# A hybrid decoder trunk on one core: half-precision pairs in the input projection from the second block on, and one small product in two halves

## The chip, the cores and the metric

The kernel runs on one core of one Trainium2 chip, as one launch. The metric is its device time in microseconds: 3231.13 us before the change, the median of three runs (3227.33 to 3232.68).

The core has five engines with queues of their own: TensorE (PE, its weight loads shown apart as PEld), VectorE (DVE), ScalarE (ACT), GpSimd (POOL) and SyncE (SP, which here only issues DMAs).

## What is computed

Two layers over 2048 tokens of width 1024, both with a pre-RMSNorm and a residual: a Mamba-2 mixer, then latent attention. The change touches the Mamba-2 mixer alone:

```python
proj = h @ w_in                                   # (2048, 1024) @ (1024, 5152)
z, xBC, dt_raw = jnp.split(proj, [D_INNER, D_INNER + CONV_DIM], axis=-1)
xBC = jax.nn.silu(causal_depthwise_conv(xBC, conv_w, conv_b))
xs, Bm, Cm = jnp.split(xBC, [D_INNER, D_INNER + SSM_GROUPS * SSM_STATE], axis=-1)
dt = jax.nn.softplus((dt_raw + dt_bias).astype(jnp.float32))
...
y_intra = jnp.einsum('btsg,btsgh,bsgh,bsghp->btghp', CB, L, dt_c, x_c)
y_inter = jnp.einsum('btgn,bghpn,btgh->btghp', C_c, state, jnp.exp(cum))
...
y = y.reshape(Bsz, S, D_INNER) * jax.nn.silu(z.astype(jnp.float32))
```

`h` is the normalised input; `L` are the decays inside a chunk. 32 heads of 64 channels in 4 groups, a state of 128, float32 in and out.

## The kernel before

**Tiling.** The tokens go in 4 blocks `b` of 512 (`TB`), the 32 heads in 4 groups `g` of 8; a block has 4 chunks `c` of 128 tokens. The width of 1024 is 8 tiles `k` of 128 rows (`KD`).

**Three matmuls for a product.** Operands of large products are kept as a pair, high part and rest, each in fp32r. `mm3` (lines 85 to 87) adds high x high, high x low and low x high. `split` (108 and 109; with a scale 111 and 112) makes such a pair: ACT copies into the high part, DVE subtracts. `pair16` (116 and 117) does the same in float16 and is used in the attention part.

**The projection of a pair (b, g).** `xbc` has two sweeps, B and C (2 banks) and x (4 banks); `zgate` has one (4 banks). Each takes 8 weight tiles from memory (`wraw`, three buffers), splits each (`wsp`, six buffers) and issues the three matmuls of 512 columns per bank and tile. So the weights are loaded and split anew in each block. `prep` turns the normalised input by PE transposes (line 171) and splits it into `xT`; `steps` makes the step sizes dt, with their own small weights (line 427).

**The scan of a pair (b, g).** `ssd` goes through 4 chunks: a transpose and a product for B and C, the decays (`E`, tile `big`, times the masked product), `Xd` = x times dt, then eight fp32 matmuls `E x Xd`, one for each head (line 549), then the state's part (`Ct` with the old state `Sp`), the new state (`Bt` with `Xp`), the gate and the turn into `yT`. The low halves of Xp, Ct and Sp are subtracted on POOL (line 500). `outp` multiplies `yT` with the output weights.

**Order.** `mamba` interleaves: while the scan of (b, g) runs, PE gets the output product of the pair before and the projection of the pair after, cut into pieces between which the scan's steps are drawn. The last group but one of a block also brings `prep` and `steps` of the next block. A scheduler then orders the instructions of each engine; weight preparation is drawn ahead by a priority (`AHEAD`).

Of the kernel before, what the change touches and what calls it, by code (L numbers as in the profile page):

```python
# [20 lines left out]
P = 128  # L21
T = 2048
D = 1024
# [45 lines left out]
class Net:  # L69
# [54 lines left out]

    def wunit(self, src, n, scale=None, late=False):

        with self.tc.high_priority(AHEAD):
            raw = self.raw(late)
            self.nc.sync.dma_start(raw[:, :n], src)
            if late:  # L130
                self.turn = not self.turn
                w = [self.t(self.sp, f"st{2 * self.turn + i}", [P, TB], F32R, bufs=1) for i in range(2)]
            else:
                u = self.t(self.wp, "wsp", [P, 2, TB], F32R, bufs=WSP)
                w = [u[:, i, :] for i in range(2)]
            self.split(w[0][:, :n], w[1][:, :n], raw[:, :n], scale)
        return w

# [47 lines left out]
    def layer_constants(self, cp):  # L186
# [13 lines left out]
        nc.vector.memset(self.mk[:, P:], NEG)  # L200
        self.wdt = cp.tile([P, KD, 2, H], F32R, name="wdt")
        self.split(self.wdt[:, :, 0], self.wdt[:, :, 1], wdt[:, :KD * H].rearrange("p (k c) -> p k c", k=KD))
# [21 lines left out]
    def mamba(self, cp):  # L224
# [9 lines left out]
        for n, (b, g) in enumerate(items):  # L234
# [81 lines left out]
    def prep(self, b, gain=None, tag="tr", each=4):  # L316
# [3 lines left out]
        for k in range(KD):  # L320
# [4 lines left out]
            if k % each == each - 1:  # L325
                yield

    def xbc(self, b, g):

        nc, w_in, xT = self.nc, self.a["ssm_w_in"], self.xT[b]  # L330
        outs = []
        for chans, tag, bufs in (([16 + g, 20 + g], "BC", 4), ([4 * g + j for j in range(4)], "xs", 8)):
            banks = [self.t(self.pp, "mm", [P, TB], bufs=4) for _ in chans]

            def weights(k):
                rows = slice(k * P, (k + 1) * P)
                if tag == "xs":
                    return self.wunit(w_in[rows, DI + g * 512:DI + (g + 1) * 512], 512)
                both = w_in[rows, DI + DI:DI + DI + 1024].rearrange("p (n q c) -> p n q c", n=2, q=G)
                with self.tc.high_priority(AHEAD):  # L340
                    raw = self.t(self.wp, "wraw", [P, TB], bufs=WRAW)
                    nc.sync.dma_start(raw[:, :256].rearrange("p (n c) -> p n c", n=2), both[:, :, g, :])
                    w = self.t(self.wp, "wsp", [P, 2, TB], F32R, bufs=WSP)
                    w = [w[:, n, :256] for n in range(2)]
                    self.split(*w, raw[:, :256])
                return w
# [24 lines left out]
    def zgate(self, b, g):  # L371

        nc, xT = self.nc, self.xT[b]
        banks, out = [self.t(self.pp, "mm", [P, TB], bufs=4) for _ in range(4)], []

        def weights(k):
            return self.wunit(self.a["ssm_w_in"][k * P:(k + 1) * P, g * 512:(g + 1) * 512], 512)

# [4 lines left out]
        def evacuate(bank, i):  # L383
            sz = self.t(self.sp, "sz", [P, TB], bufs=SZ)
            nc.scalar.activation(sz, bank, AF.Tanh, scale=0.5)
            nc.vector.scalar_tensor_tensor(sz, sz, 1.0, bank, ALU.add, ALU.mult)
            out.append(sz)
# [32 lines left out]
    def steps(self, b):  # L420

        nc, v, xT = self.nc, self.nc.vector, self.xT[b]
        ps = self.t(self.pp, "tr", [P, TB], bufs=4)

        for k in range(KD):
            for n in range(2):
                nc.tensor.matmul(ps[0:2 * H, :], self.wdt[:, k].rearrange("p n h -> p (n h)"), xT[k][:, n, :],
                                 start=k + n == 0, stop=k + n == KD)
        wk = self.t(self.sp, "big", [P, D], bufs=2)
        rt = self.t(self.sp, "yt", [2 * H, TB], bufs=2)  # L430
        nc.scalar.activation(rt, ps[0:2 * H, :], AF.Copy)
        ps = self.t(self.pp, "tr", [P, TB], bufs=4)
# [50 lines left out]
    def ssd(self, b, g):  # L483
# [21 lines left out]
        for c in range(4):  # L505
# [41 lines left out]
            for h in range(8):  # L547
                hc = slice(h * 64, (h + 1) * 64)
                nc.tensor.matmul(yi[:, hc], E[:, h, :], Xd[:, hc], start=True, stop=True)  # L549
            v.tensor_tensor(y, y, yi, ALU.add)  # L550
# [19 lines left out]
            yield  # L570
            v.tensor_tensor(y, y, szs[c], ALU.mult)
            junk = self.t(self.sp, "yt", [P, TB], bufs=2)
# [546 lines left out]
    def run(self):  # L1119
        tc = self.tc  # L1120
        with ExitStack() as whole:
# [72 lines left out]
```

## Time and profile before

| | |
|---|---|
| median of three runs | 3231.13 us |
| profiled execution | 3232.49 us |
| its span | 3230.7 us |
| Mamba-2 part, first chunk to last (86.8 to about 1620 us) | about 1530 us |
| a pair (b, g) | 83 to 113 us |

The profile is of one execution. A row of a group reads: line of the kernel, engine, operation, tile written <- tiles read, shape, count, then busy time in us and the mean duration in ns, then the engine's idle time ahead of it. A matmul's recorded duration is longer than its share of PE's time, since the next one starts before it ends; what a matmul costs in a row of them is the time from start to start (its pitch). `128*128` is the part of the array that it uses (rows * columns). One fp32 matmul stands as two, one for each of its passes.

### The profile page before, as it was taken

What the parts mean: (1) busy time and instruction counts of PE and PEld (TensorE: products, weight loads), DVE (VectorE), ACT (ScalarE), POOL (GpSimd) and SP (SyncE); (2) the same over time, 40 slices, a digit from 0 to 9 for tenths busy, and PEclk for the clock granted to TensorE, in tenths of its full rate; (3) what the DMA queues carried; (4) which work ended last, traced back from release to release, by engine and by line L of the source; (5) the groups of instructions that cost most, each with busy time, mean ns of one, the idle gap of its engine ahead of it and who ended that gap; (6) DMA issues with size and microseconds to landing.
All of it is one profiled execution on the core that took longest, in us unless ns stands there. A gap on an engine that the chain in (4) does not pass through costs nothing.

```text
span 3230.7 us, 50468 instructions
## 1 busy us (share of the span) xinstructions
PE 3152.1 (98%) x16708; PEld 2559.6 (79%) x16708; DVE 2597.2 (80%) x5490; ACT 2058.5 (64%) x5115; POOL 641.7 (20%) x846
## 2 busy tenths in 40 slices
PE   8999999999999999999999999999999999999998
PEld 6788888888888888788888888777777777777787
DVE  6888888888889888888876765678888888888675
ACT  5666666656567666576655554567777778778522
POOL 1221112221222212222111211222212221222100
PEclk9999999999999999999999999999999999999999
DMA  5333334333433334333466666854443534444385
GB/s 174 106 98 97 119 122 132 100 92 122 142 98 102 97 114 146 124 106 104 129 229 213 234 206 206 247 135 81 84 80 78 100 76 89 79 89 113 83 279 164
DMA packets 210054, 418.90 MB, mean 130 GB/s; under 512 B 27104, under 2 KB 68832, under 8 KB 208352
## 3 DMA queue, kind: packets, MB, share of 16 engines
q1 hardware_dynamic: 168032, 290.34, 29.4%
q0 software_dynamic: 41760, 125.34, 16.0%
q8 instruction: 132, 2.16, 0.3%
q14 instruction: 130, 1.06, 0.1%
HBM read 321.33 MB, written 94.24 MB: 129 GB/s over the span
## 4 chain that ended last, share of the span: by engine, by line
PE 58%; DVE 10%; ACT 4%; DMA 3%; issue 2%; SPq 0%; POOL 0%; ACTq 0%; DVEq 0%
PE mm L85 11%; PE mm L87 11%; PE mm L86 11%; PE tr L937 6%; PE tr L947 3%; PE tr L948 3%; PE tr L85 3%; PE tr L86 3%; PE tr L87 3%; DVE cacc L362 2%; PE tr L549 2%; DVE wsp L109 1%; ACT Pr L922 1%; DMA os<-ri_d 1%; DVE big L528 1%
## 5 line engine op out<-in xcount | busy, mean ns | idle before, releaser
L117 DVE SCALAR_TENSOR_TENSOR PTs<-tr,PTs 128x512 f16<-128x512 f32 (+3 forms) x640 | 374.7, 607 | 93.9 <-ACT PTs L116 87.7
L116 ACT ACTIVATE PTs<-tr 128x512 f16<-128x512 f32 (+3 forms) x640 | 328.6, 541 | 140.2 <-PE tr L937 139.4
L910 DVE TENSOR_REDUCE mx<-mm 128x1 f32<-128x512 f32 (+2 forms) x631 | 375.4, 607 | 45.4 <-PE mm L87 42.7
L922 ACT ACTIVATE Pr<-mm,nm 128x512 f32<-128x512 f32 (+2 forms) x631 | 395.4, 636 | 23.1 <-DVE nm L914 21.4
L108 ACT ACTIVATE wsp<-wraw 128x512 fp32r<-128x512 f32 (+1 forms) x452 | 252.1, 574 | 173.6 <-PE mm L87 77.4
L109 DVE TENSOR_TENSOR wsp<-wraw,wsp 128x512 fp32r<-128x512 f32 (+1 forms) x452 | 301.1, 678 | 68.0 <-ACT wsp L108 67.7
L85 PE MATMUL mm<-xT,wsp 128*128 128x512 f32 x800 | 321.2, 402 | 0.0
L937 PE MATMUL tr<-pack,Pr 128*128 128x128 f32 x2176 | 317.5, 273 | 2.0 <-ACT Os L954 1.9
L87 PE MATMUL mm<-xT,wsp 128*128 128x512 f32 x800 | 313.9, 392 | 0.0
L86 PE MATMUL mm<-xT,wsp 128*128 128x512 f32 x800 | 313.3, 392 | 0.0
L85 PE MATMUL mm<-K,xT 96*128 96x512 f32 (+2 forms) x639 | 286.7, 449 | 23.7 <-ACT Pr L922 22.7
L937 PEld LDWEIGHTS tr<-pack,Pr 128*128 128x128 f32 x2176 | 253.3, 141 | 50.4 <-ACT Os L954 2.7
L85 PE MATMUL mm<-wsp,xT 128*128 128x512 f32 (+1 forms) x640 | 242.4, 379 | 0.1
L86 PE MATMUL mm<-wsp,xT 128*128 128x512 f32 (+1 forms) x640 | 237.8, 372 | 0.0
L87 PE MATMUL mm<-wsp,xT 128*128 128x512 f32 (+1 forms) x640 | 237.5, 372 | 0.0
L87 PE MATMUL mm<-K,xT 96*128 96x512 f32 (+2 forms) x639 | 231.6, 362 | 0.0
L86 PE MATMUL mm<-K,xT 96*128 96x512 f32 (+2 forms) x639 | 231.1, 362 | 0.0
L362 DVE SCALAR_TENSOR_TENSOR cacc<-craw,pack,cacc 128x512 f32<-128x512 f32 x288 | 217.4, 776 | 16.6 <-ACT cacc L360 16.0
L542 ACT ACTIVATE Xw<-tr,d_wend 128x64 f32<-128x64 f32 x512 | 183.4, 359 | 66.0 <-DVE Xd L538 57.5
L500 POOL TENSOR_TENSOR Xp<-Xw,Xp 128x512 fp32r<-128x512 f32 x64 | 83.0, 1297 | 708.2 <-ACT Xp L499 426.0
L947 PE MATMUL tr<-PTs,xT 128*128 128x512 f16 (+3 forms) x640 | 222.0, 348 | 0.1
L948 PE MATMUL tr<-PTs,xT 128*128 128x512 f16 (+3 forms) x640 | 219.4, 347 | 0.0
(370 smaller groups left out, 8139.5 us busy)
## 6 DMA issues: line engine op xcount, KB each, us to landing
wraw<-in_ssm_w_in_dram SPq DMA_DIRECT2D x256, 256.0 KB, 2.8
big<-cumT SPq DMA_DIRECT2D x64, 512.0 KB, 4.3
wraw<-in_ssm_w_out_dram SPq DMA_DIRECT2D x128, 256.0 KB, 2.6
wraw<-in_ssm_w_in_dram SPq DMA_DIRECT2D x129, 128.0 KB, 2.3
xT<-qn_d POOLq DMA_DIRECT2D x64, 256.0 KB, 4.5
K<-kn_d POOLq DMA_DIRECT2D x15, 1024.0 KB, 9.3
wraw<-in_mla_w_uq_dram SPq DMA_DIRECT2D x36, 256.0 KB, 4.5
hx<-in_x_dram SPq DMA_DIRECT2D x16, 512.0 KB, 4.8
```

The lines of the kernel that those rows point to most:

```text
L85: mm(out, l_hi, r_hi, start=start, stop=False)
L86: mm(out, l_hi, r_lo, start=False, stop=False)
L87: mm(out, l_lo, r_hi, start=False, stop=stop)
L109: nc.vector.tensor_tensor(lo, src, hi.bitcast(F32), ALU.subtract)
L116: self.nc.scalar.activation(hi, src, AF.Copy, scale=scale)
L117: self.nc.vector.scalar_tensor_tensor(lo, src, scale, hi, ALU.mult, ALU.subtract)
L362: nc.vector.scalar_tensor_tensor(acc, raw[:, k:k + TB], wk[k], acc, ALU.mult, ALU.add)
L910: v.tensor_reduce(mx[:, n:n + 1], s[:, :w], AX.X, ALU.max)
L922: nc.scalar.activation(x[:, :w], s[:, :w], AF.Exp, bias=nm, accum_out=sm[:, n:n + 1])
L937: nc.tensor.transpose(pt[:, j * P:(j + 1) * P], st["P"][j][kb], self.ident)
L947: nc.tensor.matmul(st["O"][:, c], vals[h][:, kb, :], u[:, 0], start=kb == 0, stop=False)
L948: nc.tensor.matmul(st["O"][:, c], vals[h][:, kb, :], u[:, 1], start=False, stop=kb == nk - 1)
```

## The change

**Half-precision pairs.** In block 0 the projection stays as it was, and while its weights go by, the sum of squares of each weight row is taken: an ACT Square with a row sum ahead of each split (`dt_norm` does it for the dt columns on DVE). `row_scale` makes a power of two for each row of the weights (`rw`) and the matching gain for the input (`xg`), with one factor for the whole (`un`, `unh`) that brings the products back. From block 1 on, `prep16` writes the input, and `wpair` the weights, as float16 pairs, two tiles `k` in one buffer. In block 1 `wpair` makes them from the loaded weights and stores them to memory (`w16_d`); in blocks 2 and 3 it only loads them. `dt_pair` does the same for the dt weights. The evacuations multiply by `un` or `unh`, and so does the gate in the scan.

At the end of block 0 the output product moves behind the projection, and `row_scale` stands ahead of `prep16`.

**The product inside a chunk.** Each of the eight `E x Xd` matmuls is issued as two, with 64 columns of `E` each, which write partitions 0 to 63 and 64 to 127.

```diff
+            if norm is not None:
+                self.nc.scalar.activation(w[1][:, :n], raw[:, :n], AF.Square, accum_out=norm)
             self.split(w[0][:, :n], w[1][:, :n], raw[:, :n], scale)
...
+    def wpair(self, b, g, at, n, k, src):
+        nc = self.nc
+        if k % 2 == 0:
+            with self.tc.high_priority(AHEAD):
+                u = self.w16 = self.t(self.wp, "wsp", [P, 2, 2, n], F16, bufs=WSP)
+                kept = self.w16_d[k * P:(k + 2) * P, g, at:at + 2 * n].rearrange(
+                    "(j p) (s c) -> p j s c", j=2, s=2)
+                if b == 1:
+                    for j in range(2):
+                        raw = self.t(self.wp, "wraw", [P, TB], bufs=WRAW)
+                        src(k + j, raw)
+                        self.pair16(u[:, j, 0], u[:, j, 1], raw[:, :n], self.rw[:, k + j:k + j + 1])
+                    nc.gpsimd.dma_start(kept, u)
+                else:
+                    nc.sync.dma_start(u, kept)
+        u = self.w16
+        return [u[:, k % 2, i, :] for i in range(2)]
...
+    def row_scale(self):
...
+        v.tensor_reduce(n, self.nrm, AX.X, ALU.add)
...
+        nc.tensor.transpose(ps[0:1, 0:P], m, self.ident)
...
+        nc.tensor.matmul(ps[:, 0:2], self.ones[0:1, :], r, start=True, stop=True)
...
+    def dt_pair(self, b):
...
+                self.pair16(w[:, k, 0], w[:, k, 1], raw[:, k * H:(k + 1) * H], self.rw[:, k:k + 1])
+            nc.gpsimd.dma_start(self.wdt_d, w.rearrange("p k n h -> p (k n h)"))
...
-                parts += [self.prep(b + 1, self.g0), self.steps(b + 1)]
+                if b == 0:
+                    parts = parts[1:] + parts[:1] + [self.row_scale()]
+                parts += [self.prep16(b + 1), self.steps(b + 1)]
                 total += 3
+            elif b == 0 and g == 1:
+                self.dt_norm()
...
+    def prep16(self, b):
...
+            if k % 2 == 0:
+                u = self.t(self.xq, "xT", [P, 2, 2, TB], F16, bufs=8)
+            w = u[:, k % 2]
+            self.pair16(w[:, 0, :], w[:, 1, :], ps, self.xg[:, k:k + 1])
...
+                if b:
+                    return self.wpair(b, g, 1024 if tag == "xs" else 2048, n, k, load)
...
+                    nc.scalar.activation(w[1], raw[:, :n], AF.Square, accum_out=self.nrm[:, k, at:at + 1])
...
-                nc.scalar.activation(raw[:, 3:], bank, AF.Copy)
+                nc.scalar.activation(raw[:, 3:], bank, AF.Copy, scale=self.un if b else 1.0)
...
+            if b:
+                return self.wpair(b, g, 0, 512, k, load)
...
-                nc.tensor.matmul(yi[:, hc], E[:, h, :], Xd[:, hc], start=True, stop=True)
+                for t in (slice(0, 64), slice(64, P)):
+                    nc.tensor.matmul(yi[t, hc], E[:, h, t], Xd[:, hc], start=True, stop=True)
...
-            v.tensor_tensor(y, y, szs[c], ALU.mult)
+            if b:
+                v.scalar_tensor_tensor(y, y, self.un, szs[c], ALU.mult, ALU.mult)
+            else:
+                v.tensor_tensor(y, y, szs[c], ALU.mult)
```

Three places in the order of instructions. First PE, in the middle of a chunk of block 1, before the change: the projection's last matmuls, the decays times `Xd` (eight fp32 matmuls in one row), the state's part, and the projection again.

```order
L85 MATMUL mm_5925<-xT_3570,wsp_6009 128x512
L86 MATMUL mm_5925<-xT_3570,wsp_6009 128x512
L87 MATMUL mm_5925<-xT_3570,wsp_6009 128x512
L549 MATMUL tr_6021<-Xd_5976,big_5942 128x64 x8
L85 MATMUL tr_6031<-Sp_5860,Ct_5950 128x512
L86 MATMUL tr_6031<-Sp_5860,Ct_5950 128x512
L87 MATMUL tr_6031<-Sp_5860,Ct_5950 128x512
L85 MATMUL mm_5924<-xT_3578,wsp_6040 128x512
```

And such a place after it:

```order
L87 LDWEIGHTS wsp_6321
L87 MATMUL mm_6250<-xT_3798,wsp_6321 128x512
L683 MATMUL tr_6346<-Xd_6301,big_6267 64x64 x16
L85 MATMUL tr_6364<-Sp_6185,Ct_6275 128x512
L86 MATMUL tr_6364<-Sp_6185,Ct_6275 128x512
L87 MATMUL tr_6364<-Sp_6185,Ct_6275 128x512
L85 LDWEIGHTS wsp_6371
L85 MATMUL mm_6249<-xT_3824,wsp_6371 128x512
```

The eight matmuls have become sixteen of 64x64 in the same place, the two halves of a head behind each other; the float16 weight loads have rows of their own, which fp32r loads had not.

Second PE, at the end of block 0 after the change, around the two PE steps of `row_scale` (`rm`, a column of maxima, turned; `rr`, the factors, spread over all partitions). Between the first two and the last three rows lie matmuls of the output product like those shown.

```order
L87 MATMUL tr_3739<-Xp_3673,Bt_3578 128x512
L200 MATMUL tr_3761<-pack,rm_3759 1x128
L85 MATMUL mm_3964<-wsp_3970,yT_2960 128x512
...
L87 MATMUL mm_3964<-wsp_4058,yT_2960 128x512
L210 MATMUL tr_3771<-rr_684_3763,ones 128x2
L264 MATMUL tr_3778<-pack,hx_2709 128x128
```

The scale's two steps on PE stand 25 matmuls of the output product apart, and behind the second one come the transposes of block 1's input.

Third POOL, in block 0's last group, where the projection of block 1 begins, after the change (`w_d` is the store of pairs).

```order
L633 TENSOR_TENSOR Xp_4297<-Xw_4256,Xp_4297 128x512
L483 COPY halo<-craw_4372 128x3
L483 COPY halo<-craw_4401 128x3
L633 TENSOR_TENSOR Sp_4347<-st_761_4137,Sp_4347 128x512
L633 TENSOR_TENSOR Ct_4731<-BC_2949,Ct_4731 128x128
L481 COPY craw_4638<-halo 128x3
L481 COPY craw_4667<-halo 128x3
L156 DMA w_d<-wsp_4499 128x2x1024
L633 TENSOR_TENSOR Xp_4533<-Xw_4480,Xp_4533 128x512
L156 DMA w_d<-wsp_4561 128x2x1024
L633 TENSOR_TENSOR Ct_5006<-BC_4410,Ct_5006 128x128
```

The stores stand between the low halves that the scan's matmuls read; before the change this queue had only those and the halo copies here.

More of the change, by code (lines that the diff above doesn't have):

```diff
@@ L123, in raw, with wunit @@
         return self.t(self.sp, self.raws[0], [P, TB], bufs=2)
-    def wunit(self, src, n, scale=None, late=False):
+    def wunit(self, src, n, scale=None, late=False, norm=None):
         with self.tc.high_priority(AHEAD):
@@ new lines, in dt_pair @@
+    def dt_pair(self, b):
+        nc = self.nc
+        w = self.t(self.wp, "wraw", [P, KD, 2, H], F16, bufs=WRAW)
+        if b == 1:
+            raw = self.t(self.wp, "wraw", [P, TB], bufs=WRAW)
+            self.load_dt(raw)
+            for k in range(KD):
+                self.pair16(w[:, k, 0], w[:, k, 1], raw[:, k * H:(k + 1) * H], self.rw[:, k:k + 1])
+            nc.gpsimd.dma_start(self.wdt_d, w.rearrange("p k n h -> p (k n h)"))
+        else:
+            nc.sync.dma_start(w.rearrange("p k n h -> p (k n h)"), self.wdt_d)
@@ L200, in layer_constants @@
         nc.vector.memset(self.mk[:, P:], NEG)
-        self.wdt = cp.tile([P, KD, 2, H], F32R, name="wdt")
+        self.wdt = self.t(self.wp, "wsp", [P, KD, 2, H], F32R, bufs=WSP)
+        self.nrm = cp.tile([P, KD, 3 * G + 1], F32, name="nrm")
+        self.rw = cp.tile([P, KD], F32, name="rw")
+        self.xg = cp.tile([P, KD], F32, name="xg")
+        self.un = cp.tile([P, 1], F32, name="un")
+        self.unh = cp.tile([P, 1], F32, name="unh")
         self.split(self.wdt[:, :, 0], self.wdt[:, :, 1], wdt[:, :KD * H].rearrange("p (k c) -> p k c", k=KD))
@@ L326, in prep @@
                 yield
+    def prep16(self, b):
+        xs = self.xn.pop(b)
+        self.xT[b] = []
+        for k in range(KD):
+            ps = self.transposed(xs, k)
+            if k % 2 == 0:
+                u = self.t(self.xq, "xT", [P, 2, 2, TB], F16, bufs=8)
+            w = u[:, k % 2]
+            self.pair16(w[:, 0, :], w[:, 1, :], ps, self.xg[:, k:k + 1])
+            self.xT[b].append(w)
+            if k % 4 == 3:
+                yield
     def xbc(self, b, g):
@@ L333, in xbc, with load, weights @@
             banks = [self.t(self.pp, "mm", [P, TB], bufs=4) for _ in chans]
-            def weights(k):
+            def load(k, raw):
                 rows = slice(k * P, (k + 1) * P)
                 if tag == "xs":
-                    return self.wunit(w_in[rows, DI + g * 512:DI + (g + 1) * 512], 512)
-                both = w_in[rows, DI + DI:DI + DI + 1024].rearrange("p (n q c) -> p n q c", n=2, q=G)
+                    nc.sync.dma_start(raw, w_in[rows, DI + g * 512:DI + (g + 1) * 512])
+                else:
+                    both = w_in[rows, DI + DI:DI + DI + 1024].rearrange("p (n q c) -> p n q c", n=2, q=G)
+                    nc.sync.dma_start(raw[:, :256].rearrange("p (n c) -> p n c", n=2), both[:, :, g, :])
+            def weights(k):
+                n = 512 if tag == "xs" else 256
+                if b:
+                    return self.wpair(b, g, 1024 if tag == "xs" else 2048, n, k, load)
                 with self.tc.high_priority(AHEAD):
                     raw = self.t(self.wp, "wraw", [P, TB], bufs=WRAW)
-                    nc.sync.dma_start(raw[:, :256].rearrange("p (n c) -> p n c", n=2), both[:, :, g, :])
+                    load(k, raw)
                     w = self.t(self.wp, "wsp", [P, 2, TB], F32R, bufs=WSP)
-                    w = [w[:, n, :256] for n in range(2)]
-                    self.split(*w, raw[:, :256])
+                    w = [w[:, i, :n] for i in range(2)]
+                    at = 3 * g + (1 if tag == "xs" else 2)
+                    nc.scalar.activation(w[1], raw[:, :n], AF.Square, accum_out=self.nrm[:, k, at:at + 1])
+                    self.split(*w, raw[:, :n])
                 return w
@@ L384, in evacuate @@
             sz = self.t(self.sp, "sz", [P, TB], bufs=SZ)
-            nc.scalar.activation(sz, bank, AF.Tanh, scale=0.5)
+            nc.scalar.activation(sz, bank, AF.Tanh, scale=self.unh if b else 0.5)
             nc.vector.scalar_tensor_tensor(sz, sz, 1.0, bank, ALU.add, ALU.mult)
@@ L423, in steps @@
         ps = self.t(self.pp, "tr", [P, TB], bufs=4)
+        w = self.dt_pair(b) if b else self.wdt
         for k in range(KD):
             for n in range(2):
-                nc.tensor.matmul(ps[0:2 * H, :], self.wdt[:, k].rearrange("p n h -> p (n h)"), xT[k][:, n, :],
+                nc.tensor.matmul(ps[0:2 * H, :], w[:, k].rearrange("p n h -> p (n h)"), xT[k][:, n, :],
                                  start=k + n == 0, stop=k + n == KD)
@@ L430, in steps @@
         rt = self.t(self.sp, "yt", [2 * H, TB], bufs=2)
-        nc.scalar.activation(rt, ps[0:2 * H, :], AF.Copy)
+        nc.scalar.activation(rt, ps[0:2 * H, :], AF.Copy, scale=self.un[0:2 * H] if b else 1.0)
         ps = self.t(self.pp, "tr", [P, TB], bufs=4)
@@ L1137, in run @@
             self.wv_d = dp.tile([256, 1024], F32, name="wv_d")
+            self.wdt_d = dp.tile([P, KD * 2 * H], F16, name="wdt_d")
+            self.w16_d = dp.tile([D, G, 2560], F16, name="w16_d")
             self.us_d = dp.tile([1024], F32, name="us_d")
```

51 lines of the change are left out of this document (50 added, 1 removed).

## Prediction

> **What bounds the kernel now.** I read the page's engine totals first, then the stretches of the blocks, then what TensorE (PE) waits for in them, and last the timeline of one chunk.
>
> ```profile
> span 3230.7 us, 50468 instructions
> PE 3152.1 (98%) x16708; PEld 2559.6 (79%) x16708; DVE 2597.2 (80%) x5490; ACT 2058.5 (64%) x5115; POOL 641.7 (20%) x846
> ...
> PEclk9999999999999999999999999999999999999999
> ```
>
> PE is busy for 98% of the span at an undisturbed clock. Matmuls overlap in this record, so a busy PE alone proves little; the next view settles it. It lists the stretches of blocks 0 and 1 (from the first chunk of each to that of the next).
>
> ```profile
> core 0: us, PE busy (x) PEld busy (x) DVE busy (x) ACT busy (x) POOL busy (x), PEclk, DMA share, GB/s
> 86.80:463.10 376.30, 372.77 (x1853) 307.00 (x1852) 327.45 (x658) 245.35 (x625) 79.47 (x90) 1.00 0.35 105
> 463.10:858.50 395.40, 391.56 (x1932) 323.46 (x1931) 340.36 (x681) 247.95 (x622) 83.43 (x97) 1.00 0.37 113
> ```
>
> PE stands still for 3.5 and 3.8 us; DVE runs at 87% and 86%, ACT at 65% and 63%. Here are all of PE's waits between 375 and 1547 us, in which every projection of blocks 1 to 3 lies (columns: total, times, longest).
>
> ```profile
> PE tr L549 <- DVE big L530: 5.2, 7, 1.5
> PE tr L549 <- issue: 3.5, 1, 3.5
> PE tr L171 <- DVE st L567: 2.7, 2, 1.4
> PE tr L549 <- DVE Xd L538: 2.2, 1, 2.2
> PE tr L576 <- DVE xT L109: 2.0, 1, 2.0
> ```
>
> 15.6 us in 1172. So the Mamba part is bound by PE's own stream of instructions: each nanosecond taken off a matmul there is a nanosecond off the end, and work taken off DVE or ACT can return at most those 15.6 us. The attention part behind it is untouched.
>
> **Half-precision projection, blocks 1 to 3.** A pair (block, group) has 8 x (2 + 4 + 4) x 3 = 240 matmuls of 128x512; twelve pairs make 2880, the same number after as before, in f16 instead of fp32r. These are the groups of the projection between 463 and 1448 us, and then the only f16 matmuls of this width in the trace, in the attention part.
>
> ```profile
> L85 PE MATMUL mm<-xT,wsp 128*128 128x512 f32 x480 | 192.7, 402 | 0.0
> L87 PE MATMUL mm<-xT,wsp 128*128 128x512 f32 x480 | 188.4, 392 | 0.0
> L86 PE MATMUL mm<-xT,wsp 128*128 128x512 f32 x480 | 187.6, 391 | 0.0
> ...
> L85 PE MATMUL mm<-wsp,xT 128*128 128x512 f32 x320 | 128.0, 400 | 0.1
> ...
> L87 PE MATMUL mm<-wsp,xT 128*128 128x512 f32 x320 | 125.4, 392 | 0.0
> L86 PE MATMUL mm<-wsp,xT 128*128 128x512 f32 x320 | 125.2, 391 | 0.0
> ```
>
> ```profile
> L947 PE MATMUL tr<-PTs,xT 128*128 128x512 f16 x448 | 170.1, 380 | 0.1
> L948 PE MATMUL tr<-PTs,xT 128*128 128x512 f16 x448 | 169.8, 379 | 0.0
> ```
>
> (192.7 + 188.4 + 187.6) / 1440 = 0.3949 us and (128.0 + 125.4 + 125.2) / 960 = 0.3944 us against 0.3795 us: 15 ns each. Durations hold the same pipeline tail, so their difference is a difference of pitch. The timeline of a chunk in block 1 gives the pitch itself:
>
> ```profile
> 599.87 0.39 PE L85 MATMUL mm<-xT,wsp 128*128 128x512 f32 x1
> ...
> 600.55 0.39 PE L85 MATMUL mm<-xT,wsp 128*128 128x512 f32 x1
> ...
> 601.00 0.39 PE L87 MATMUL mm<-xT,wsp 128*128 128x512 f32 x1
> 601.00 1.98 PEld L549 LDWEIGHTS tr<-Xd,big 128*128 128x128 f32 x16
> ...
> 601.23 1.89 PE L549 MATMUL tr<-Xd,big 128*128 128x64 f32 x16
> ...
> 602.93 0.47 PE L85 MATMUL tr<-Sp,Ct 128*128 128x512 f32 x1
> ```
>
> ```profile
> 2281.58 0.38 PE L947 MATMUL tr<-PTs,xT 128*128 128x512 f16 x1
> 2281.80 0.38 PE L948 MATMUL tr<-PTs,xT 128*128 128x512 f16 x1
> 2282.02 0.27 PE L937 MATMUL tr<-pack,Pr 128*128 128x128 f32 x1
> ```
>
> fp32r: (601.00 - 599.87) / 5 = 0.226 us. f16: (2282.02 - 2281.58) / 2 = 0.22, two digits only. The pitch of undisturbed pairs says 6 to 11 ns, the means say 15; the rest is that L85 is 8 to 10 ns longer on average than L86 and L87: now and then it starts late, because an fp32r load is exposed behind a transpose or an fp32 product, and the short f16 load should not be. So the term lies between 2880 x 6 = **-17** and 2880 x 17 = **-49 us**; I take the means, 2880 x 15.3 = **-44 us**. Nothing else can end later in its place, since PE hardly waits here.
>
> **Decays times x in halves.** Per chunk, 8 heads of fp32 with two passes, 16 pairs of a 128-column load and a 64-column matmul, become 32 pairs with 64-column loads. By the rows above the group now lasts from 601.23 to the real start of the next matmul, 602.93 + 0.08 (that one is 0.47 long where 0.39 is usual): 1.78 us, 0.111 a pair, and 64 x 1.78 = 114 us in the kernel. What sets 0.111? Recorded loads by width:
>
> ```profile
> L427 PEld LDWEIGHTS tr<-xT,wdt x64: 132/134/138, 21.2 to 1143.1; 128*64 128x64 f32 x64
> ...
> L549 PEld LDWEIGHTS tr<-Xd,big x1024: 186/192/333, 86.6 to 1595.7; 128*128 128x128 f32 x171
> ```
>
> 64 columns fewer shorten a load by 58 ns, so 128 columns cost about twice that, 0.11 us: the pitch. The group is bound by its loads; the matmuls lie in their shadow. Loads of half the width should follow each other at about 0.056 us, and 32 x 0.056 = 1.79 us: **nothing gained, nothing lost**, if loads go one after another. Can pairs be issued that closely?
>
> ```profile
> 2285.28 0.22 PE L947 MATMUL tr<-PTs,xT 128*128 128x128 f16 x1
> 2285.34 0.22 PE L948 MATMUL tr<-PTs,xT 128*128 128x128 f16 x1
> ```
>
> Yes, 0.06 us apart, each with its load. The trace shows no two tiles at work side by side, so both ends stay open. Best: the loads of the two halves run together, 0.028 us a pair, 0.9 us a chunk, 64 x 0.89 = -57 us. Worst: a pair keeps its 0.111 us and there are twice as many, 64 x 1.78 = +114 us. I take 0, by the nearest row (L427, whose loads are these in width and tile), and keep both ends.
>
> Switching the array from whole to half and back comes 64 x 2 times. The one switch the trace has, from L427's 128*64 tile to the whole array:
>
> ```profile
> 21.67 3.63 PE L427 MATMUL tr<-xT,wdt 128*64 128x512 f32 x15
> 25.14 0.39 PE L87 MATMUL mm<-xT,wsp 128*128 128x512 f32 x1
> 25.37 0.39 PE L85 MATMUL mm<-xT,wsp 128*128 128x512 f32 x1
> ```
>
> L87 starts 0.16 us before the last L427 has ended (21.67 + 3.63 = 25.30), exactly as L85 starts 0.16 before L87 ends (25.53 - 25.37): no drain to be seen, 0 taken. The Trainium skill, "TensorEngine Tiling (Array Packing)", Key Properties, says that changing the tiling mode drains TensorE. By that rule each of 128 switches would lay open about 0.16 us, 20 us in all, and the forecast would be 3209; by this row it costs nothing.
>
> **What the other engines get.** Durations from these rows:
>
> ```profile
> L573 ACT ACTIVATE yt<-y 128x512 f32<-128x512 f32 x64 | 40.3, 630 | 60.1 <-DVE y L571 59.9
> ...
> L573 ACT ACTIVATION_READ_ACCUMULATOR yt<-y 128x1 f32 x64 | 11.9, 186 | 0.0
> ```
>
> ```profile
> L109 DVE TENSOR_TENSOR wsp<-wraw,wsp 128x512 fp32r<-128x512 f32 x324 | 239.4, 750 | 50.6 <-ACT wsp L108 50.3
> ...
> L112 DVE SCALAR_TENSOR_TENSOR wsp<-wraw,pack,wsp 128x512 fp32r<-128x512 f32 x136 | 107.2, 792 | 6.5 <-ACT wsp L111 6.4
> ```
>
> Block 0: each of its 96 weight tiles gets a Square with a row sum, 0.82 us at 512 columns. 72 of them fall into the stretch of block 0, at most 59 us on 245: ACT goes from 65% to 81%, still hidden behind PE. The first 24 lie in the start-up, where weights are on the path: 0 to 20 us, I take **+4**. Block 1: pairs with a row scale cost DVE 0.042 us more per tile (792 against 750), 96 x 0.042 = 4 us over 395, hidden. Its 48 stores of pairs and one of dt are issued by POOL, whose queue holds behind each the low halves of Xp, Ct and Sp and the halo copies.
>
> ```profile
> L779 POOL DMA_DIRECT2D kn_d<-big x15 | 10.2, 681 | 20.0 <-DVE big L109 16.2 <-DVE rsq L152 3.9
> ```
>
> 49 x 0.68 = 33 us on POOL's 83 of 395; PE reads Xp twelve or more matmuls after the group (2.6 us), which covers it: 0 taken, +33 if every issue came through to PE. Blocks 2 and 3: 192 tiles need no split (at 0.75 us, at most 144 us less for DVE); of the 15.6 us of waits I give back **-2**. An f16 pair has the bytes of the fp32 tile that it replaces, so these loads move what they moved; the pairs of block 1 are written once, 21 MB, on DMA engines that are 37% busy. The scale step's one round trip over PE, at the end of block 0, has 25 matmuls between its two PE instructions (25 x 0.23 = 5.8 us) for twelve DVE operations, two of them splits of 0.79 us: 0.
>
> **Sum.** -44 + 0 + 4 - 2 = -42 us. The profiled execution took 3232.49 us (span 3230.7 and 1.8 around it); 3232.5 - 42 = 3190.5. It was 1.4 us over the median 3231.13, so the forecast is **3189 us**.
>
> **The rivals.**
> *Halves at work together* (27%): both halves' loads overlap; 3189 - 57 = **3132**, anything between being a partial overlap. For it: they use different columns and write different partitions. Against it: loads in the trace never run two at a time, and each head's two passes use the same half in turn, so the other half stands behind them in the queue.
> *A pair has a fixed price* (15%): a load can't go under the matmul before it in half-array mode, or the issue of a two-pass fp32 pair costs as much at half the width: 3189 + 114 = **3303**, slower than now. It decides from 0.111 / 2 + 42 / 2048 = 0.076 us a pair on: there the projection's gain is eaten up. Against it: L427's 64-column loads do lie under running matmuls (15 in 3.63 us).
> The Trainium skill, "TensorE: Matmul & The Clock Gate", Part 3, The mechanism, states that a load overlaps matmuls in flight only where the row group differs; these halves share all rows, so it would make load and matmul follow each other, and speaks for this rival. L427's rows disagree with it.
> *f16 gains nothing here* (7%): the pitch stays at 0.226, because the moving operand and not the type sets it, and the sum is that of the small terms: 3231 + 4 - 2 = **3233**, no change. Against it: L947 and L948.
>
> **How the numbers follow.** Forecast and its neighbourhood 3170 to 3215 have 45%; overlap 27% (3125 to 3170); fixed price 15%; no gain 7%; late Xp from POOL's stores, or drains, 6% (3209 to 3228). The range 3125 to 3228 leaves out the fixed price and a little more. A measurement can tell 0.2% from no change, 6.5 us. Faster: 45 + 27 + 5 = 77%; same 7%; slower 16%.
>
> **What would show it.** Right: projection matmuls of 0.380 us in blocks 1 to 3, blocks 2 and 3 with DVE near 70%, and a 64x64 group of 1.8 us a chunk with loads near 0.134. The group at 0.9 or at 3.5 us decides between the rivals. Wrong in the small terms: PE waiting for Xp behind POOL in block 1, or for wsp in block 0.

## The result, and the profile after

The changed kernel takes 3212.05 us (median of four runs, 3210.4 to 3213.47) against 3231.9 us (four runs, 3227.33 to 3236.62): a ratio of 0.9942, 95% interval 0.993 to 0.9954. It is faster by 0.6%, 20 us, where the forecast had 42.

The page of the changed kernel, its totals and clock:

```profile
span 3208.6 us, 52002 instructions
PE 3101.7 (97%) x17735; PEld 2245.6 (70%) x17735; DVE 2511.8 (78%) x5330; ACT 2024.2 (63%) x5123; POOL 661.9 (21%) x895
...
PEclk9999999999999999999999999999999999999999
```

PE has 50 us less to do (3152.1 before), the span is 22 us shorter. So 28 us of what PE was relieved of came back as time in which PE stands still. The stretches of the four blocks say where (from the first decays product of a block to that of the next; the last ends at the last chunk):

```profile
core 0: us, PE busy (x) PEld busy (x) DVE busy (x) ACT busy (x) POOL busy (x), PEclk, DMA share, GB/s
87.40:468.10 380.70, 368.28 (x2112) 271.96 (x2111) 333.97 (x690) 281.74 (x761) 90.87 (x103) 1.00 0.39 118
468.10:865.70 397.60, 376.00 (x2187) 224.10 (x2186) 333.25 (x656) 243.75 (x597) 106.51 (x133) 0.99 0.47 153
865.70:1241.70 376.00, 369.99 (x2187) 222.80 (x2186) 290.25 (x584) 205.44 (x528) 75.45 (x97) 1.00 0.36 116
1241.70:1567.40 325.70, 315.27 (x1894) 198.62 (x1893) 256.14 (x493) 176.77 (x468) 73.00 (x85) 0.99 0.40 128
```

The same view of blocks 2 and 3 before the change:

```profile
858.50:1251.80 393.30, 389.57 (x1931) 322.37 (x1930) 340.08 (x681) 250.88 (x624) 87.28 (x97) 1.00 0.36 110
1251.80:1594.20 342.40, 334.38 (x1653) 278.26 (x1652) 290.81 (x565) 210.78 (x539) 78.51 (x85) 0.99 0.39 123
```

Blocks 0 and 1 took 376.3 and 395.4 us before: both are now a little **longer**, with PE idle for 12.4 and 21.6 us where it was 3.5 and 3.8. Blocks 2 and 3 are shorter by 17.3 and 16.7. There DVE has 50 and 35 us less to do (it is busy for 77% of block 2, 86% before); in block 1 it has 7 us less, in block 0 6.5 us more. PE's busy time fell in all four.

What PE waits for in blocks 1 to 3, the nine largest entries (columns: total, times, longest):

```profile
PE tr L683 <- DVE big L663: 9.5, 8, 2.4
PE tr L86 <- POOL Xp L633: 5.2, 11, 0.9
PE tr L683 <- DVE Xd L671: 4.8, 4, 2.3
PE tr L264 <- DVE st L701: 4.8, 2, 3.3
PE mm L85 <- ACT craw L482: 4.4, 6, 1.5
PE tr L713 <- DVE xT L109: 2.8, 1, 2.8
PE tr L85 <- ACT Xp L632: 2.3, 1, 2.3
PE mm L85 <- DVE hs L545: 1.6, 1, 1.6
PE mm L85 <- DVE sz L518: 1.1, 2, 0.8
```

They make 36.5 us of 37.6 in 1100, against 15.6 in 1172 before; 24.6 of the 36.5 end with something from DVE. No weight tile is among them: most of these 24.6 us end with operands of the scan (`big`, `Xd`, `st`), which stand in the same DVE queue as the weights' conversions.

The projection's groups of matmuls, between 468 and 1430 us:

```profile
L85 PE MATMUL mm<-xT,wsp 128*128 128x512 f16 x480 | 182.9, 381 | 0.0
L87 PE MATMUL mm<-xT,wsp 128*128 128x512 f16 x480 | 182.4, 380 | 0.0
L86 PE MATMUL mm<-xT,wsp 128*128 128x512 f16 x480 | 182.3, 380 | 0.0
...
L85 PE MATMUL mm<-wsp,xT 128*128 128x512 f16 x320 | 121.4, 379 | 4.4 <-ACT craw L482 4.4
L87 PE MATMUL mm<-wsp,xT 128*128 128x512 f16 x320 | 121.3, 379 | 0.0
L86 PE MATMUL mm<-wsp,xT 128*128 128x512 f16 x320 | 121.3, 379 | 0.0
```

911.6 us for 2400 is 0.3798 each, where 0.3947 stood: 15 ns less, as forecast. Counted from start to start over the rows of the projection without a wait, the mean fell from 233 to 217 ns.

And the timeline around one product of decays and x in block 1:

```profile
566.47 0.39 PE L86 MATMUL mm<-wsp,yT 128*128 128x512 f32 x1
566.70 0.40 PE L87 MATMUL mm<-wsp,yT 128*128 128x512 f32 x1
567.03 1.15 PE L683 MATMUL tr<-Xd,big 128*64 128x64 f32 x32
568.11 0.50 PE L85 MATMUL tr<-Sp,Ct 128*128 128x512 f32 x1
...
567.02 1.01 PEld L683 LDWEIGHTS tr<-Xd,big 128*64 128x64 f32 x32 [0.37 <-issue]
```

The 32 pairs start between 567.03 and 567.96: 0.93 us where 1.78 was forecast. Taken from the start of the matmul ahead (566.70) to the real start of the one behind (568.11 + 0.10, since that one is 0.50 long where 0.40 is usual), the group costs 1.51 us; in the chunk shown of before it was 603.01 - 601.00 = 2.01. That is 0.50 us a chunk, 32 us in 64 chunks. It is no single case: over all chunks whose group neither follows a wait nor is followed by one, the median fell from 2.24 us (51 chunks, from the start of the matmul ahead to that of the second one behind) to 1.73 (44 chunks). The rival "halves at work together" has come true in good part. The records of the first pairs give the two halves side by side (starts in us, from the trace):

```
matmuls  567.026 567.033 | 567.133 567.140 | 567.191 567.198 | 567.250 567.256 | 567.308 567.315 ...
loads    567.025 567.031 | 567.080 567.086 | 567.135 567.142 | 567.194 567.200 | 567.252 567.259 ...
```

Two loads start 6 ns apart and each lasts 0.13 to 0.14 us; a couple comes every 58 ns.

PE was thus offered more than the forecast gave it, about 32 us from the halves beside the 40 from float16, and the kernel made less of it. The experiments ask where it went.

### The profile page after: what moved, and what is told of

It reads as the page before. It is cut to its first block, busy times and chain, and to the rows that moved or that the text cites. A ratio compares the mean times of both kernels' runs of the same rounds, so it can differ in the third digit from the quotient of the medians.

```text
span 3208.6 us, 52002 instructions
## 1 busy us (share of the span) xinstructions
PE 3101.7 (97%) x17735; PEld 2245.6 (70%) x17735; DVE 2511.8 (78%) x5330; ACT 2024.2 (63%) x5123; POOL 661.9 (21%) x895
## 4 chain that ended last, share of the span: by engine, by line
PE 62%; DVE 17%; ACT 7%; DMA 6%; issue 6%; POOL 1%; SPq 1%; ACTq 0%; DVEq 0%; POOLq 0%
PE mm L85 12%; PE mm L87 12%; PE mm L86 12%; PE tr L1074 6%; DVE cacc L488 4%; PE tr L86 3%; PE tr L1084 3%; PE tr L1085 3%; PE tr L85 3%; PE tr L87 3%; DMA wraw<-in_ssm_w_in_dram 2%; DMA big<-cumT 2%; DVE big L661 1%; DVE wsp L112 1%; DMA os<-ri_d 1%
## 5 line engine op out<-in xcount | busy, mean ns | idle before, releaser
L87 PE MATMUL mm<-xT,wsp 128*128 128x512 f16 (+1 forms) x800 | 308.3, 386 | 3.5 <-DVE wsp L117 2.3
L85 PE MATMUL mm<-xT,wsp 128*128 128x512 f16 (+1 forms) x800 | 311.4, 389 | 0.0
L86 PE MATMUL mm<-xT,wsp 128*128 128x512 f16 (+1 forms) x800 | 308.1, 385 | 0.0
L675 ACT ACTIVATE Xw<-tr,d_wend 128x64 f32<-128x64 f32 x512 | 182.5, 357 | 93.5 <-DVE Xd L671 85.7
L85 PE MATMUL mm<-wsp,xT 128*128 128x512 f16 (+2 forms) x640 | 235.4, 368 | 4.5 <-ACT craw L482 4.4
L86 PE MATMUL mm<-wsp,xT 128*128 128x512 f16 (+2 forms) x640 | 234.0, 366 | 0.0
L87 PE MATMUL mm<-wsp,xT 128*128 128x512 f16 (+2 forms) x640 | 233.6, 366 | 0.0
L87 PE MATMUL mm<-K,xT 96*128 96x512 f32 (+2 forms) x639 | 231.0, 361 | 0.0
L85 PE MATMUL mm<-wsp,yT 128*128 128x512 f32 x512 | 208.5, 408 | 3.3 <-DVE hs L545 2.1
L87 PE MATMUL mm<-wsp,yT 128*128 128x512 f32 x512 | 204.3, 399 | 0.0
```

The costliest lines, as they stand in the source:

```text
L85: mm(out, l_hi, r_hi, start=start, stop=False)
L86: mm(out, l_hi, r_lo, start=False, stop=False)
L87: mm(out, l_lo, r_hi, start=False, stop=stop)
L675: act(Xw[:, hc], px[:, hc], AF.Copy, scale=wend[:, h0 + h:h0 + h + 1])
```

## The experiments

Lengths in us of the profiled run of each kernel, by the same marks as above (block 3 to its last chunk; "rest" is the output of the mixer's end and the attention part), and its median and ratio. Lengths are from one execution each and from unrounded marks, so they can differ by 0.1 from the lines shown; two executions of the changed kernel differ by up to 2.2 in a block.

| kernel | start-up | block 0 | block 1 | block 2 | block 3 | rest | median | ratio (95%) |
|---|---|---|---|---|---|---|---|---|
| before | 86.8 | 376.3 | 395.4 | 393.3 | 342.3 | 1636.5 | 3231.9 | |
| after | 87.4 | 380.7 | 397.6 | 376.0 | 325.7 | 1641.2 | 3212.05 | 0.9942 (0.993 to 0.9954) |
| after, again | 85.5 | 382.9 | 398.7 | 375.7 | 325.2 | 1641.0 | 3211.47 | 0.9937 (0.992 to 0.9953) |
| halves alone | 86.2 | 376.8 | 395.7 | 395.8 | 342.0 | 1637.8 | 3235.62 | 1.0017 (1.0007 to 1.0027) |
| pairs alone | 86.0 | 384.2 | 400.3 | 384.9 | 328.5 | 1641.8 | 3226.37 | 0.9983 (0.9973 to 0.9992) |
| stores from SP | 85.7 | 380.5 | 397.1 | 375.5 | 325.4 | 1638.7 | 3203.79 | 0.9916 (0.9899 to 0.9934) |
| no row sums | 89.2 | 384.8 | 396.8 | 376.1 | 327.8 | 1639.6 | 3213.52 | 0.9944 (0.9927 to 0.9961) |
| four raw buffers | 86.6 | 382.2 | 394.9 | 376.3 | 324.1 | 1637.5 | 3203.7 | 0.9907 (0.9893 to 0.9922) |
| tile by tile | 86.6 | 385.4 | 398.5 | 376.1 | 324.2 | 1642.0 | 3210.46 | 0.9934 (0.9919 to 0.9949) |
| pairs made in every block | 86.7 | 379.4 | 393.2 | 393.2 | 340.9 | 1638.0 | 3237.41 | 1.0016 (1.0007 to 1.0025) |
| ... no low parts (DVE) | 86.1 | 378.0 | 373.7 | 377.0 | 333.1 | 1637.8 | 3184.27 | 0.9854 (0.9831 to 0.9877) |
| ... no high parts (ACT) | 86.4 | 378.5 | 392.3 | 392.8 | 334.8 | 1640.1 | 3227.82 | 0.999 (0.9979 to 1.0) |
| ... no loads | 85.5 | 380.3 | 385.4 | 385.7 | 334.3 | 1638.3 | 3211.84 | 0.9939 (0.9919 to 0.9959) |
| four raw buffers, stores from SP | 86.1 | 379.2 | 395.2 | 377.1 | 326.5 | 1635.2 | 3196.69 | 0.9889 (0.9872 to 0.9905) |

### Each part of the change alone

The halves put into the kernel before:

```diff
-                nc.tensor.matmul(yi[:, hc], E[:, h, :], Xd[:, hc], start=True, stop=True)
+                for t in (slice(0, 64), slice(64, P)):
+                    nc.tensor.matmul(yi[t, hc], E[:, h, t], Xd[:, hc], start=True, stop=True)
```

> The kernel before, with only the decays-times-x product in two halves. The trace of the change shows the group from the matmul ahead of it to the first one behind it take 1.52 us a chunk (566.70 to 568.22) where 2.01 stood before (601.00 to 603.01), so 64 x 0.49 = 32 us are to be had. Theory A (the halves gain, the losses belong to the half-precision pairs): 3232 - 32 = 3200, range 3192 to 3206. Rival (a shorter group takes the cover from what stands behind it on PE, Xp and the state's part, and the time comes back as waits): 3215 to 3232, with PE waiting for Xp on POOL and ACT in all blocks.

And the changed kernel with that edit undone:

```diff
-                for t in (slice(0, 64), slice(64, P)):
-                    nc.tensor.matmul(yi[t, hc], E[:, h, t], Xd[:, hc], start=True, stop=True)
+                nc.tensor.matmul(yi[:, hc], E[:, h, :], Xd[:, hc], start=True, stop=True)
```

> The changed kernel with the product in one piece again, so the half-precision pairs alone. Theory A (pairs gain 45 us on PE, and their preparation in blocks 0 and 1 costs about 55 us of waits): 3212 + 32 = 3244, not faster than before; range 3232 to 3250. Rival (the two parts share the loss, since each takes cover from the other): below 3225, so that pairs alone are a gain too.

Halves alone: 1.0017, slightly slower. The stretches of blocks 1 and 2 of this kernel:

```profile
462.90:858.60 395.70, 386.01 (x2187) 310.73 (x2186) 340.11 (x681) 246.70 (x622) 83.80 (x97) 0.99 0.37 113
858.60:1254.40 395.80, 384.63 (x2187) 309.53 (x2186) 339.75 (x681) 248.75 (x624) 83.11 (x97) 1.00 0.36 110
```

PE has 5.6 and 4.9 us less to do than in the kernel before (391.56 and 389.57), stands still for 9.7 and 11.2 instead of 3.8 and 3.7, and the blocks are as long as they were (395.4 and 393.3), to 2.5 us. What PE waits for there:

```profile
PE tr L550 <- DVE big L530: 9.0, 6, 1.7
PE tr L171 <- DVE st L568: 6.2, 2, 3.2
```

These two are 15.2 of 20.8 us, where 7.5 stood before: a wait of PE for DVE has taken the place of PE's work. Neither expectation was met. The whole kernel did not fall to 3192 to 3206, and the waits that came are for DVE, with 1.8 us for Xp on POOL, which the rival had named.

Pairs alone, 3226.37, lie between the two expectations (3232 to 3250, or below 3225). Blocks 2 and 3 together are shorter by 22.2 us for the 7 projections that they hold, 22.2 / (7 x 240) = 13 ns a matmul, the float16 term; block 0 longer by 7.9 and block 1 by 4.9. The same halves are worth 384.9 - 376.0 = 8.9 us in block 2 when it comes with pairs, the full 16 x 0.50 = 8, and nothing in block 2 of the kernel before. What differs is whether DVE still converts weights there. That is one theory, **DVE's queue as a second bound, level with PE**; its rivals are the row sums on ACT, the stores on POOL, the way the pairs of block 1 are made two at a time, and the three raw buffers.

### Stores from SP

```diff
-                    nc.gpsimd.dma_start(kept, u)
+                    nc.sync.dma_start(kept, u)
```

> The changed kernel with the stores of the pairs in block 1 issued by SP and not by POOL. If POOL's queue is what PE waits for in block 1 (Xp, Ct and Sp low halves behind 48 stores of 0.73 us), block 1 falls from 398 us towards 375 and the time to about 3190. If it is ACT and DVE, within 4 us of 3212; or longer, since SP's loads then stand behind stores that wait for DVE: up to 3230.

Block 1 keeps its length (397.1), so POOL's queue is not what stretches it. Yet the whole is 8 us shorter than the changed kernel (3203.79 and 3212.05), twice what was allowed for that case. The profiled runs, 5.9 us apart, put 2.5 into the rest and 1.7 into the start-up; no single place explains it.

### No row sums

```diff
-            if norm is not None:
-                self.nc.scalar.activation(w[1][:, :n], raw[:, :n], AF.Square, accum_out=norm)
...
-                self.dt_norm()
+                nc.vector.memset(self.nrm, 1.0)
...
-                    nc.scalar.activation(w[1], raw[:, :n], AF.Square, accum_out=self.nrm[:, k, at:at + 1])
```

> The changed kernel without the 96 Squares with row sums in block 0 and without the sums of the dt columns; the sums are set to one, so all rows have the same scale. The stretch of block 0 is 381 us where its PE work without waits would give about 364 (376 before, 8 less by the halves, 4 less by the first half-precision projection). If ACT's extra 70 us are what holds block 0, it falls by 10 to 16 us and the time to 3196 to 3202. Rival (the order of the end of block 0, with the output product behind the projection, and the pairs of block 1 that are made there, cost it): by under 5 us, 3207 to 3212.

3213.52, and block 0 is 384.8: the 96 Squares cost nothing that shows, in block 0 or in the start-up (89.2 without them).

### Four raw buffers

The sums of squares are put where the mask of the attention part will stand, and the mask is filled in later; the space goes to a fourth `wraw`.

```diff
-WRAW = 3
+WRAW = 4
...
-        self.nrm = cp.tile([P, KD, 3 * G + 1], F32, name="nrm")
+        self.nrm = self.mk.bitcast(F32)[:, :KD * (3 * G + 1)].rearrange("p (k c) -> p k c", k=KD)
...
```

> The changed kernel with four buffers for raw weights instead of three (the row sums lie in the space of the attention mask, which is filled after the scale step). In block 1 ACT waits 37 us in 34 pieces for raw weights to land, 0 such entries stood among its longest before. If this wait, in ACT's queue ahead of evacuations and the scan's copies, is what costs PE its 33 us of waits in block 1 (6.6 before), block 1 falls from 398 us by 10 us or more and the time to under 3202. If the raw loads are late only because ACT and DVE are, the time stays within 5 us of the changed kernel beside it.

3203.7, where the changed kernel measured together with it has 3211.47: 8 us, of which block 1 has 3.8 and the rest 3.5 in the profiled runs. Block 1 did not fall by the 10 us that were expected of a cause, and the whole gained more than the 5 us left to the other case. The buffers are a part, not the cause.

### Tile by tile

The pair of tiles of block 1 is made one tile at a time, each ahead of its own matmuls.

```diff
-        if k % 2 == 0:
-            with self.tc.high_priority(AHEAD):
...
-                    for j in range(2):
-                        raw = self.t(self.wp, "wraw", [P, TB], bufs=WRAW)
+        with self.tc.high_priority(AHEAD):
+            if k % 2 == 0:
+                self.w16 = self.t(self.wp, "wsp", [P, 2, 2, n], F16, bufs=WSP)
+            u, j = self.w16, k % 2
...
+            if b == 1:
+                raw = self.t(self.wp, "wraw", [P, TB], bufs=WRAW)
+                src(k, raw)
+                self.pair16(u[:, j, 0], u[:, j, 1], raw[:, :n], self.rw[:, k:k + 1])
+                if j:
...
```

> The changed kernel with the weights of block 1 made tile by tile, each where it is needed, and not two at every second tile. If the bunching of two loads and two conversions is the cause, block 1 falls by 10 us or more, and so does the last group of block 0 (85 us); the time goes to under 3202. If the amount of work on ACT and DVE is the cause, it stays within 5 us of the changed kernel beside it.

3210.46, block 1 398.5: making them in couples costs nothing that shows.

### Pairs made in every block

Nothing is stored or loaded back; blocks 2 and 3 convert the weights as block 1 does. Float16 and halves stay.

```diff
-                if b == 1:
+                if b:
...
-                    nc.gpsimd.dma_start(kept, u)
-                else:
-                    nc.sync.dma_start(u, kept)
```

> The changed kernel in which blocks 2 and 3 make their pairs as block 1 does, and nothing is stored. It measures two things. Block 1 without the 48 stores: if the stores cost it, it falls from 398 us by 10 us or more; else it stays at 393 to 400. Blocks 2 and 3 with conversions: if the relief of DVE and ACT is what lets PE's gains through, block 2 goes from 376 to 393 us or more and the kernel to 3235 to 3250; if PE's own shorter stream were the bound there, block 2 stays under 382.

Beside these the changed kernel was measured once more:

> The changed kernel once more, as the neighbour of the three others on the same chip: 3212, range 3204 to 3218.

The whole gain is gone: 3237.41, 1.0016 of the kernel before, though PE has all that both parts of the change save it. Its blocks 1 and 2:

```profile
466.20:859.40 393.20, 375.67 (x2189) 224.01 (x2188) 346.71 (x681) 257.59 (x623) 82.64 (x97) 0.99 0.37 114
859.40:1252.50 393.10, 376.62 (x2187) 224.95 (x2186) 346.87 (x681) 259.54 (x625) 82.59 (x97) 0.99 0.36 111
```

393 us, as before the change, with DVE at 88%. What DVE stands idle for, from 466 to 1210 us:

```profile
DVE y L681 <- ACT y L673: 27.7, 12, 3.6
DVE wsp L117 <- ACT wsp L116: 14.5, 24, 1.4
DVE st L697 <- POOL Sp L630: 9.7, 10, 1.2
```

These are the three largest; all such waits make 85 of its 89 idle us. So DVE's missing 12% are waits of its next instruction for another engine or a transfer. That they hold up work behind it which could have run is argued, not shown.

The stores have to be read by groups, since in the changed kernel the last group of block 1 already projects with ready pairs, and here it does not. The three groups of block 1 whose projections convert (from the first product of decays and `Xd` of each to that of the next) take 98.9 + 98.9 + 115.3 = 313.1 us in the changed kernel and 314.3 in its second execution, 307.0 here without stores, and 291.3 in the changed kernel's block 2 with ready pairs. So conversions cost block 1 about 16 us and the stores 6 to 7; with the stores from SP the three take 312.6.

### Which step of the conversion

Three kernels take one step of the conversion out of the last one: the low parts, which DVE subtracts; the high parts, which ACT copies; the loads of the weights.

```diff
-                        self.pair16(u[:, j, 0], u[:, j, 1], raw[:, :n], self.rw[:, k + j:k + j + 1])
+                        nc.scalar.activation(u[:, j, 0], raw[:, :n], AF.Copy, scale=self.rw[:, k + j:k + j + 1])
...
-        return [u[:, k % 2, i, :] for i in range(2)]
+        return [u[:, k % 2, 0, :], self.zero[:, :n]]
...
```

> As the kernel without stores, whose blocks 1 to 3 all make their pairs (393, 393 and 341 us to the last chunk), but DVE does not subtract the low parts of the projection's weights in them: a tile of zeros stands for the low part, and PE, ACT and the loads do what they did. DVE loses 96 operations or some 65 us of work a block. Theory D (DVE's queue is the second bound): block 2 falls from 393 to 376 to 380 us, as if the pairs were only loaded. Theory A (ACT's queue) and theory L (the loop of three raw buffers): it stays above 388; by L a little less, since a raw buffer then comes free a step earlier.

```diff
-                        self.pair16(u[:, j, 0], u[:, j, 1], raw[:, :n], self.rw[:, k + j:k + j + 1])
+                        nc.vector.scalar_tensor_tensor(u[:, j, 1], raw[:, :n], self.rw[:, k + j:k + j + 1], self.zero[:, :n],
+                                                       ALU.mult, ALU.subtract)
...
-        return [u[:, k % 2, i, :] for i in range(2)]
+        return [self.zero[:, :n], u[:, k % 2, 1, :]]
...
```

> As the kernel without stores, but ACT does not copy the high parts of the projection's weights in blocks 1 to 3: a tile of zeros stands for the high part, and DVE subtracts zero from the scaled weights, so its work stays. ACT loses some 60 us of work a block, and with it its waits for raw weights. Theory A: block 2 falls from 393 to 376 to 380 us. Theory D: it stays above 388. By theory L it falls in part, 380 to 390, since a raw buffer is free one step earlier.

```diff
-                        raw = self.t(self.wp, "wraw", [P, TB], bufs=WRAW)
-                        src(k + j, raw)
+                        raw = self.pack[:, 0:2 * P].unsqueeze(1).to_broadcast([P, n // (2 * P), 2 * P])
...
```

> As the kernel without stores, but the projection's weights in blocks 1 to 3 are not loaded: ACT and DVE convert a constant tile in their place, as many operations of the same size. Theory L (the loads through three raw buffers, behind which ACT stands in its queue): block 2 falls from 393 to 376 to 382 us. Theories D and A: it stays above 388.

Block 1 of each. Without the low parts:

```profile
464.10:837.80 373.70, 369.71 (x2187) 222.79 (x2186) 288.02 (x584) 255.91 (x623) 74.25 (x97) 1.00 0.38 119
```

Without the high parts:

```profile
464.80:857.10 392.30, 374.29 (x2187) 223.02 (x2186) 348.26 (x681) 203.23 (x526) 83.46 (x97) 1.00 0.37 114
```

Without the loads:

```profile
465.80:851.20 385.40, 372.73 (x2187) 222.95 (x2186) 342.52 (x681) 253.57 (x623) 78.76 (x97) 1.00 0.18 61
```

The second number is the length, the fifth DVE's busy time. Taking 59 us off **DVE** shortens the block by 19.5 us, to what PE's own stream takes (4.0 us idle), with every load and every ACT copy still there; over the kernel it is 3237.41 to 3184.27 (46 us between the profiled executions). Taking 54 us off **ACT** shortens it by 0.9. Taking away the **loads** shortens it by 8 at nearly the same work on DVE: the loop of a raw buffer (load, copy, subtraction, buffer free) accounts for a part, perhaps the same that the fourth buffer touches. Block 2 gives 377.0, 392.8 and 385.7: the first is what was expected for DVE's queue, the second speaks against ACT's, and the third lies between what the two kinds of theory allowed. In block 3 the three kernels gain alike (340.9 to 333.1, 334.8 and 334.3), so there they don't part the theories. In blocks 1 and 2 DVE's subtractions are the main cause; how much of it is sheer work, how much is order in its queue and how much the loop of the raw buffers these runs don't part.

### The two small mends together

The fourth raw buffer and the stores from SP, both as shown above, in the changed kernel.

> The changed kernel with both edits that gained alone, four raw buffers (3204 beside 3211) and the stores issued by SP (3204 in another set, where the changed kernel had 3212 in its own). If they gain in different places, 3195 to 3200; if both loosen the same queue, 3201 to 3206.

3196.69 us, 0.9889 of the kernel before (0.9872 to 0.9905): shorter than with either mend alone, and what was expected if they gain in different places (3195 to 3200). Where each gains stays open.

## Why the prediction was right and wrong

**Direction and float16: right.** The forecast took 15.3 ns a matmul from the means; the means now say 14.9, and blocks 2 and 3 of the kernel with pairs alone delivered 13. By that the term of -44 is -38, in a stretch where the end follows PE's own stream. The upper bound of 17 ns rested on no row.

**The halves: the term of 0 was mis-sized,** and the rival at 27% was nearly right. The step that failed is "if loads go one after another", with its witness L427. They go two at a time: 0.058 us for two where L427's loads and the 0.111 of before gave 0.056 for one. The sentence that loads never run two at a time was no reading of the rows either: the 16 loads of 192 ns in 1.98 us that the prediction shows already overlap in the records. On PE the term is -32, not -57. That rival had 0.89 us a chunk and 0.50 came. Of the 0.39 between them, 0.10 lie at the entry, 0.22 at the exit (0.25 from the last pair to the next matmul, where the rival has one more pair, 0.03), and the rest in a pair that takes 0.030 and not 0.028.

**The mode switch: costed at nothing, and it costs.** Entry: 567.03 - 566.70 = 0.33 us where the matmuls ahead follow each other at 0.23. Exit: 568.21 - 567.96 = 0.25 where the group of before had 0.16 from its last pair to the next matmul. Against the group of before that is 0.10 + 0.09 = 0.19 a chunk, 12 us in all, contained in the 0.50 above. The witness was wrong here too: L427 is in fp32r. It was not the one switch of the trace, as the prediction says. Behind it stands a small product in plain fp32, on half of the rows:

```profile
25.83 0.39 PE L87 MATMUL mm<-xT,wsp 128*128 128x512 f32 x1
26.15 0.46 PE L434 MATMUL tr<-pack,yt 64*128 64x64 f32 x4
26.53 0.50 PE L85 MATMUL mm<-xT,wsp 128*128 128x512 f32 x1
```

Its entry takes 0.32 us (it also waits for ACT there), and behind its last matmul the next one starts after 0.15 us and is 0.50 long: the same exit as that of the halves (0.15 and 0.50). In float16 the same small product as L427 (L560 after the change) shows the step:

```profile
359.32 0.47 PE L87 MATMUL mm<-wsp,yT 128*128 128x512 f32 x1
359.72 0.62 PE L560 MATMUL tr<-xT,wraw 128*64 128x512 f16 x2
```

L87 starts late by 0.08 (0.47 long for 0.39), so from its real start 0.32 us pass where 0.23 are usual. At its end, 0.42 us pass from the last start to the real start of the next matmul (0.31, and that one is 0.51 long for 0.40), so 0.19 lie open there. The drain of which the Trainium skill, "TensorEngine Tiling (Array Packing)", Key Properties, speaks is there, for the halves at somewhat over half of the 0.16 us that the prediction worked out for it. L427 shows none of it, at neither end; why is open.

**A fixed price per pair: did not come.** A pair went from 0.111 to 0.029 us. What the prediction cited for this rival from the Trainium skill, "TensorE: Matmul & The Clock Gate", Part 3, disagrees with the records above, in which loads and matmuls of halves that share all rows lie over one another.

**The step on which the forecast failed: "each nanosecond taken off a matmul there is a nanosecond off the end".** It came from PE's 15.6 us of waits, and with it "work taken off DVE or ACT can return at most those 15.6 us" and "hidden behind PE" for blocks 0 and 1. That PE hardly waited showed that the others kept up with PE as it was, not that they would keep up with a faster one. DVE, at 85 to 87% of each block, was level with PE: halves alone took 5 us of work a block off PE and nothing off the end; all of the change but the reloading of pairs ended at 3237; and taking some 58 us off DVE in each of blocks 1 and 2 there, and 41 in block 3, gave 53 us in the end. The changed kernel is faster only where it relieves **both**: in blocks 2 and 3, whose pairs come ready from memory (DVE at 77 and 79% there, where the prediction looked for about 70). The forecast counted that relief as "-2"; it is what the whole gain hangs on. That the time lies inside the range of 3125 to 3228 is luck: the halves offered 32 us that the sum had put at 0, and blocks 0 and 1 lost 39.

The account, by stretch: with 13 ns a float16 matmul and 0.50 us a chunk, PE was offered 11 us in block 0 (its 16 chunks, and the first pair of block 1, which is projected there), 21 in block 1, 21 in block 2, 17 in block 3: 70. Delivered: -4.4, -2.2, 17.3 and 16.6. Blocks 2 and 3 give 34 of 38. Blocks 0 and 1 lose 39, 23 of them in block 1: about 16 to conversions and 6 to 7 to the stores, as worked out above.

Block 0 loses 15 to 16. Its four groups took 82.5, 94.7, 111.4 and 87.6 us before and take 81.9, 89.4, 124.5 and 84.9 now; by the changed order 22 matmuls of 512 columns have moved from the second group, and 28 from the last, into the third. With 0.23 us for each of these, 2 us a group for the halves and 3 in the last for float16, the groups should take 80.5, 87.6, 120.9 and 76.1 (an estimate). So 9 of the loss lie in the last group, where the first pairs of block 1 are made: DVE is busy there for 77 of 84.9 us, and 6.1 of the 6.6 us that PE waits end with DVE. Without the stores this group takes 82.8, without the low parts as well 81.4. The first two groups lose 3 of the 4 us that the halves offer them, as the kernel with halves alone does. The third, with the row scale and `prep16`, loses about 4 and stays open; these two were not tried apart. It is not the row sums, without which block 0 takes 384.8.

**Start-up +4, POOL's stores 0.** The start-up went from 86.8 to 87.4 and 85.5: nothing. The stores, bounded by 0 and +33, cost 6 to 7 us in block 1, and not through POOL's queue; by which way stays open. The rest of the kernel, in which no instruction was edited, is 4.7 us longer (1641.2 and 1641.0 against 1636.5); with the stores from SP it is 1638.7, with four raw buffers 1637.5, with both 1635.2. Why is open, and these are single executions.

## What to carry to other kernels

When PE never waits, the next engine may still be one step behind it: before costing a saving on PE in full, look for an engine that is nearly as busy in the same stretch (here DVE, at 85 to 87%), and count the saving in full only where that engine is relieved too. An engine that waits for others in between can be full before it is 100% busy: DVE gave no more at 88% here. And a witness row for a new form of instruction must have the same type, not only the same shape.

## What the runs showed of the hardware

- Two 64-column halves of the array take fp32 weights and matmuls at the same time: loads 6 ns apart, each 0.13 to 0.14 us long, a couple every 58 ns, 0.029 us a pair against 0.111 for a whole-array pair of the same moving size.
- Going from the whole array to 64-column tiles and back laid open about 0.1 us each way in fp32, and 0.1 and 0.19 in float16 (L560); the fp32r product of 128*64 (L427) showed none of it.
- In a block of 393 us, DVE busy for 347 (88%) was level with PE: 54 us off ACT shortened it by 0.9, 59 us off DVE by 19.5.
